# A triangular inverse written earlier into the program, and SBUF pools moved to equal offsets

## The chip, the cores and the metric

The kernel runs on one core of a Trainium2 chip. A core has five engines, each with its own instruction stream: TensorE (PE in the profile; its weight loads are listed apart as PEld), VectorE (DVE), ScalarE (ACT), GpSimd (POOL) and SyncE (SP, which here only issues DMAs). Each engine works through its stream in order, and engines wait for each other on semaphores. Operands live in SBUF (128 partitions), and matmul results in PSUM, in eight banks of 128 x 512 fp32. The metric is the device time in microseconds of one execution.

## The reference: what is computed

Two layers of a diffusion backbone over 512 latent tokens and 256 context tokens with 1024 channels. Layer 0 puts a chunked gating MLP and a bidirectional RWKV-7 mixer with eight heads side by side, between one input projection and one output projection; layer 1 is a bidirectional chunkwise mLSTM. After each mixer comes a ConvFFN: an up projection to 2 x 2816 channels, a 3x3 depthwise convolution, a gated GELU and a down projection. Norms, adaLN modulation, gates and residual adds stand around each part.

The change touches the RWKV-7 recurrence, which the reference writes token by token:

```
def step(s, inp):
    r_t, w_t, k_t, v_t, kk_t, b_t = inp
    sa = jnp.einsum('bhvk,bhk->bhv', s, kk_t)
    s = s * w_t[:, :, None, :] - sa[..., None] * b_t[:, :, None, :] + v_t[..., None] * k_t[:, :, None, :]
    return s, jnp.einsum('bhvk,bhk->bhv', s, r_t)
```

It runs over context, then latent tokens, in both directions. Because each step subtracts what the state already holds along kk, a block of tokens can be done at once only with the inverse of a unit lower triangular matrix between its tokens.

The second thing that the change touches is where the tiles of the later parts lie, ConvFFN included:

```
a, b = jnp.split(h @ w_up, 2, axis=-1)
a = dwconv1d(a, conv_w[1]) if rows is None else dwconv_grid(a, conv_w, rows)
return (jax.nn.gelu(a + conv_b) * b) @ w_down
```

## The kernel before

**Stages.** Norms and adaLN rows of layer 0 (to about 140 us), its projection stage (to about 380), the chain stage of the RWKV recurrence (398 to 615), the output projection (to about 700), ConvFFN 0 (706 to 1236), the mLSTM (to about 1590) and ConvFFN 1 (to the end). Matmuls against weights are done in three passes over a high and a low part of each fp32 operand (`load_w`, L118 to L125, makes the parts: ScalarE rounds to `hi`, VectorE or GpSimd subtracts to get `lo`).

**Sets.** The eight RWKV heads are worked as four pairs of heads, called sets here and numbered ct = 0 to 3 as in the code. For each set, the projection stage makes its inputs (`prep_e`, `prep_n`), stores them to a DRAM area (`setd`, by `set_part`), and inverts its triangular 64 x 64 blocks (`prep_t`, L579 to L636).

**The inverse.** `prep_t` takes the 32 x 32 diagonal blocks by forward substitution on VectorE: 31 steps of two tensor operations each (L597 a product into `fs`, L599 an addition into `Ti`), of up to 256 elements per partition. It gives up control after every third step, that is ten times. Then come three block transposes on VectorE (`Td` L604, `Tn` L605, `On` L607), four copies on ScalarE of 32 x 768 into `TT` (L613, L614), two groups of small matmuls `w` (L621) with copies to `Wm`, two groups `t` (L630) with copies into `TT` on VectorE (L633), and a store of `TT` to DRAM (L636). It yields once behind the copies, and once behind each matmul group, so it consists of 15 pieces and the store. The scratch tiles have one buffer each: `Ai`, `Td` and `Wm` share one, `Ti` and `On` another. So the inverse of a set can begin only when the one before has used up its tiles. Sets 0 and 1 are inverted in the projection stage; sets 2 and 3 are written behind it, and use the single PSUM bank "7".

**The chain stage.** Four lanes, one per set, walk 12 steps each over the tokens. Lanes 0 and 1 run side by side, then lanes 2 and 3. Each group of 4 steps of a lane first loads its part of the set back from DRAM (`rbp`, `LB`, `ttp`, L932 to L943) and is prepared (`prep_g`: transposes, `az` products). The stage is six blocks: blocks 0 to 2 are the three groups of lanes 0 and 1, blocks 3 to 5 those of lanes 2 and 3. Beside the lanes' steps, a block weaves in the preparation of the next group; block 0 the inverse of set 2, block 1 the inverse of set 3 (`inverse()`, which at its end closes the inverse's scratch pool `tx` and opens `late0`, a pool for adaLN rows, in its place); blocks 2 to 4 the job `ada` that multiplies these rows (L157, loads L154). `finish` ends a pair of lanes.

**What sets the order.** `weave` (L302) interleaves generators: it always advances the one whose progress key is least, where a generator with weight w and start f has the key f + (1 - f)(done + 0.5)/w. This fixes the order in which the program writes its instructions. A planner of the framework then simulates the machine and gives each engine an order: among the instructions ready at a time it takes the first written one, except that the lanes' chain steps are written under a raised priority (`crit`). So an instruction written late may run early, where an engine would else be idle. On the chip the resulting order of each engine is strict. DMAs of SP's queue are issued in the same way, in a strict order.

**Pools.** SBUF is handed out from both ends: most pools grow from the left, some (`H`, `act1`, `inv0`, the weights' working tiles of the projection stage) from the right. A pool's start follows from the sizes of those before it. From the pool of the residual stream (`x`, L1142) on, the left pools `xc`, `strm` (split weights), `gatebc`, `strmr` (raw weights), `wo0` to `wo7`, `op0`, and the ConvFFN's `fhid` (hidden tiles, with the convolution's coefficients `fpar`) and `fs` (scratch) follow one another.

Of the kernel before, what the change touches and what calls it, by code (L numbers as in the profile page):

```python
# [8 lines left out]
F32 = mybir.dt.float32  # L9
# [5 lines left out]
P = 128  # L15
# [36 lines left out]
PF = _Cols()  # L52
# [17 lines left out]
def build(tc, *args, **kw):  # L70
    with ExitStack() as ctx:
        _build(ctx, tc, *args, **kw)


def _build(ctx, tc, xall, par, cst, ada_0, ada_w, ada_t, w_in, w_out, ffn_up, ffn_down, lora, wsT, a_bs, c_in, c_gate, c_out, mneg, parf, parm, out):
# [9 lines left out]
    def bank(name, role):  # L85

        turn[role] = turn.get(role, -1) + 1
        return pp.tile([P, 512], F32, tag=role[turn[role] % len(role)], name=name)
# [201 lines left out]
    def woven(*gens):  # L290

        live = [[g[0], 0, g[1], g[2] if len(g) > 2 else 0.0] for g in gens]
        while live:
            k = min(range(len(live)), key=lambda j: live[j][3] + (1 - live[j][3]) * (live[j][1] + 0.5) / live[j][2])
            try:
                next(live[k][0])
                live[k][1] += 1
            except StopIteration:
                live.pop(k)
            yield  # L300

    def weave(*gens):  # L302
        for _ in woven(*gens):
            pass

    def part_of(g, n):
        for _ in range(n):
            next(g)
            yield

    def run(gen):
        for _ in gen:
            pass
# [16 lines left out]
    with ExitStack() as lx:  # L330
# [102 lines left out]
        prbank = lambda name: bank(name, "2435")  # L433
# [9 lines left out]
        def conv_tile(col, pool, tag, name, bufs=1):  # L443
            pl, pcx = unit(col, name)
            y = pool.tile([P, T], F32, tag=tag, name=name, bufs=bufs)
            ci = col - 8
            for (a, n, src) in ((0, TC, pcx), (TC, TL, pl)):
                conv3(y[:, a:a + n], src, pc("shift0", ci), pc("shift1", ci), pc("shift2", ci), n)
            return y
# [19 lines left out]
        def set_part(ct, k):  # L469
            o = 0  # L470
            for kk_, n in SET:
                if kk_ == k:
                    return setd[ct][:, o:o + n]
                o += n
# [78 lines left out]
        def prep_n(ct):  # L553

            s = st[ct]
            RBv = s["RB"].rearrange("p (u a t) -> p u a t", a=2, t=64)
            LBv = s["LB"].rearrange("p (u a t) -> p u a t", a=2, t=64)
            NF = wkT.tile([P, 56, 32], F32, tag="NF", name=f"NF{ct}", bufs=2)
            G.memset(NF[:, 24:32], 0.0)
            G.memset(NF[:, 32:56], 0.0)  # L560
            for g8 in range(3):
                px, py = bank(f"nx{ct}{g8}", "23"), bank(f"ny{ct}{g8}", "45")
                for k in range(8):
                    u = g8 * 8 + k
                    mm(px[0:64, k * 64:k * 64 + 64], LBv[0:64, u, u // 12, :], RBv[0:64, u, 0, :], start=True, stop=True)
                    mm(py[64:128, k * 64:k * 64 + 64], LBv[64:128, u, u // 12, :], RBv[64:128, u, 0, :], start=True, stop=True)
                us = slice(g8 * 8, g8 * 8 + 8)
                for (pp, b0, e) in ((px, 0, A), (py, 64, A)):
                    p3 = pp.rearrange("p (u t) -> p u t", t=64)
                    cpy = e.copy if e is A else e.tensor_copy  # L570
                    off = slice(32 + g8 * 8, 40 + g8 * 8)
                    cpy(NF[b0:b0 + 32, us], p3[b0:b0 + 32, :, 0:32])
                    cpy(NF[b0 + 32:b0 + 64, us], p3[b0 + 32:b0 + 64, :, 32:64])
                    cpy(NF[b0 + 32:b0 + 64, off], p3[b0:b0 + 32, :, 32:64])
                yield
            for k in ("RB", "LB"):
                nc.sync.dma_start(set_part(ct, k), s[k])
            s["NF"] = NF
# [266 lines left out]
        def ada_job(jobs, pool, rawb, *how):  # L845
            for g in jobs:
                yield from ada_gen(g, pool, "7", rawb, *how)

        def kr(ct):
            st[ct] = {}  # L850
            for c0, tag in ((12, "kT"), (8, "rT")):
                st[ct][tag] = conv_tile(c0 + ct, wkP, tag, f"{tag}{ct}", 2)
                yield

        def v(ct):
            st[ct]["vT"] = conv_tile(16 + ct, wkS, "vT", f"vT{ct}")
            yield

        def chained(*gens):
            for g in gens:  # L860
                yield from g

        def start_prep(ct):
            PLt = keep.tile([P, 24], F32, name=f"PL{ct}")
            st[ct]["PL"] = PLt
            for k, n in SET:
                if k not in ("vT", "TT"):
                    st[ct][k] = wkS.tile([P, n], F32, tag=k, name=f"{k}{ct}")
            return prep_e(ct, st[ct]["kT"], st[ct]["rT"])
# [10 lines left out]
        def part(n):  # L880
            for _ in range(n):
                next(SG)
                yield

        NA = (4, 6, 6)
        run(kr(0))
        weave((start_prep(0), 8), (chained(v(0), kr(1), part(0)), 3 + 0))
        run(prep_n(0))
        for ct in range(3):
            n = NA[ct]  # L890
            weave(*([(prep_t(ct, prbank), 13, 0.0)] if ct < 2 else []), (chained(start_prep(ct + 1), prep_n(ct + 1)), 9 + 3, 0.0),
                  (chained(v(ct + 1), *([kr(ct + 2)] if ct < 2 else []), part(n)), 3 + n, 0.0))
        run(SG)
        ex.close()
        hx.close()
        rx.close()
        sx.close()
        Ts = [prep_t(ct, lambda name: bank(name, "7")) for ct in (2, 3)]
        fin = lx.enter_context(tc.tile_pool(name="fin0", bufs=1))
        ch = lx.enter_context(tc.tile_pool(name="chain0", bufs=1))  # L900
        ys = [[fin.tile([P, 2, w], F32, name=f"y{n}{w}") for w in (TC, TL)] for n in ("01", "23")]
# [43 lines left out]
        def load_bv(ct):  # L945
            t = fin.tile([P, T], F32, tag="bv", name=f"bvr{ct}", bufs=2)
            nc.sync.dma_start(t, set_part(ct, "bv"))
            st[ct]["bv"] = t
# [3 lines left out]
        def inverse():  # L952
            yield from Ts[1]
            tx.close()
            late["p"] = lx.enter_context(tc.tile_pool(name="late0", bufs=1))
            nc.scalar.dma_start(lwg, lora[:, 1024:1536])

        def preps(cts, g):
            for ct in cts:
                if g == 0:  # L960
                    load_v(ct)
                load_g(ct, g)
            for ct in cts:
                load_t(ct, g)
                yield from prep_g(ct, g)
# [7 lines left out]
        for b, (k, g) in enumerate(blocks):  # L973
            n = (22, 20, 22 - 10 * k)[g]
            todo = [(part_of(C[k], n) if g < 2 or k else C[k], n)]
            if b < 5:
                kk_, gg_ = blocks[b + 1]
                todo.append((preps(pairs[kk_], gg_), 10))
            if b == 0:
                todo.append((Ts[0], 13))  # L980
            elif b == 1:
                todo.append((inverse(), 13))
            elif b < 5:
                todo.append((part_of(ada, (5, 6, 5)[b - 2]), (5, 6, 5)[b - 2]))
            if b == 3:
                for ct in range(2):
                    load_bv(ct)
                todo.append((finish((0, 1), ys[0], ("01", "01"), "ctx"), 8))
            elif b == 4:
                todo.append((finish((0, 1), ys[0], ("01", "01"), "lat"), 8))  # L990
            elif b == 5:
                todo.append((finish((2, 3), ys[1], ("01", "01"), "ctx"), 8))
            weave(*todo)
            if g < 2:
                run(part_of(C[k], 4))
            if b == 1:
                ada = ada_job([1, 2], late["p"], 2, 2048)
            if b == 2:
                C.append(chains(pairs[1], ys[1]))
            if b == 4:  # L1000
                run(ada)
                gate_rows(0, 0, "7")
                scale_vec(0, 1)
                load_bv(2)
                load_bv(3)
# [53 lines left out]
    def ffn(l, xt, hT, ctx_too, after, final=None, beneath=None):  # L1059

        with ExitStack() as fx:
            hidp = fx.enter_context(tc.tile_pool(name=f"fhid{l}", bufs=1))
            hid = [hidp.tile([P, NH, w], F32, tag=f"hid{g}", name=f"hid{l}{g}") for g, w in ((0, TL), (1, TC))[:2 if ctx_too else 1]]
            fpar = hidp.tile([P, PF.n], F32, name=f"fpar{l}")
            nc.scalar.dma_start(fpar, parf[l])
            sp = fx.enter_context(tc.tile_pool(name=f"fs{l}", bufs=1))
            fill = beneath(sp) if beneath else None
# [71 lines left out]


    strm.sub, strm.hi, strm.lo = nc.vector, 3, 3
    xp = ctx.enter_context(tc.tile_pool(name="x", bufs=1))  # L1142
    H = {tg: ctx.enter_context(tc.tile_pool(name=f"H{tg}", bufs=1, side="right")) for tg in ("lat", "ctx")}
    xcx = ExitStack()
# [56 lines left out]
    def beneath(pool):  # L1201
# [6 lines left out]
        return ada_sums(rows, place)  # L1208

    ffn(0, xt, hT, True, to_layer1, None, beneath)  # L1210


# [396 lines left out]
```

## Time and profile before

| what | value |
|---|---|
| median of three runs | 1970.32 us (1968.26 to 1972.65) |
| the profiled execution | 1975.72 us, with a span of 1973.8 us from the first to the last instruction |
| mean granted TensorE clock | 0.965 of full speed |
| TensorE busy | 1854.0 us, 94% of the span |
| VectorE busy | 1334.4 us, 68% |
| ScalarE busy | 800.1 us, 41% |
| GpSimd busy | 306.9 us, 16% |
| DMA | 227.77 MB, mean 115 GB/s |

How to read the views: a row of the timeline has the start in us, the duration, the engine, the line of the kernel, the operation, the output and input tiles (without set and buffer numbers), the shapes, and how many instructions are drawn together; in brackets stands the idle time of the engine before it and what ended that. A row of a group of instructions has the busy time and the mean duration in ns, then the idle time in front and what ended most of it. In a table of stretches, each engine has its busy time and, in brackets, its instructions; then come the granted clock of TensorE (PEclk, 1.00 is full speed), the share of time that the DMA engines moved data, and their rate. SPq rows are DMA issues on SP's queue.

### The profile page before, as it was taken

The page shows a single profiled execution, that of the slowest core. Times are in us where ns is not written, and L with a number is a line of the kernel's source. Part 1 is how long each engine was busy: PE and PEld are TensorE (multiplying, and loading weights), DVE is VectorE, ACT ScalarE, POOL GpSimd, SP SyncE. Part 2 cuts the span into 40 slices and gives each one's busy share as a digit, 9 for nine tenths or more (in the row PEclk, how much of TensorE's full clock was granted, in tenths as well). Part 3 has the DMA queues.
Part 4 walks back from the last instruction along what each step waited for, and adds up shares of the span by engine and source line. Part 5 has one row for each costly group of instructions (what it writes and reads, how often), then busy time and mean ns, then how long its engine had stood idle before and what let it go on. Part 6 is the DMA issues. An engine that isn't in the chain of part 4 may idle for free.

```text
span 1973.8 us, 31872 instructions
## 1 busy us (share of the span) xinstructions
PE 1854.0 (94%) x12411; PEld 1508.3 (76%) x12411; DVE 1334.4 (68%) x2669; ACT 800.1 (41%) x1429; POOL 306.9 (16%) x429
## 2 busy tenths in 40 slices
PE   6998789698898999999999998999999989999998
PEld 4777677587666888888888886778888768888886
DVE  4379675757345589999994337667777688777534
ACT  4364645534335442222222226475554353323222
POOL 2222222311000222223330002100110020000001
PEclk9999889788899999999999999999999999999999
DMA  7133121643764524444432224431111312222222
GB/s 292 54 123 123 57 103 55 182 123 83 204 184 138 182 99 160 150 160 165 161 134 76 97 96 160 151 92 44 33 43 44 139 56 96 96 96 96 88 94 86
DMA packets 102887, 227.77 MB, mean 115 GB/s; under 512 B 28224, under 2 KB 44048, under 8 KB 99664
## 3 DMA queue, kind: packets, MB, share of 16 engines
q1 hardware_dynamic: 100976, 222.26, 33.4%
q10 hardware_dynamic: 1760, 3.47, 0.5%
q8 instruction: 98, 1.61, 0.3%
q14 instruction: 53, 0.43, 0.1%
HBM read 199.31 MB, written 26.39 MB: 114 GB/s over the span
## 4 chain that ended last, share of the span: by engine, by line
PE 58%; DVE 2%; POOL 1%; ACT 1%; issue 1%; DMA 0%; DVEq 0%; SPq 0%; ACTq 0%; POOLq 0%
PE of L1044 5%; PE of L1043 5%; PE of L1045 5%; PE pl_fb L268 4%; PE pl_fb L266 4%; PE pl_fb L267 4%; PE pl_fa L267 4%; PE pl_fa L268 4%; PE pl_fa L266 4%; PE pd L1453 1%; PE pe L1430 1%; PE kv L1386 1%; PE pc_fa L267 1%; PE pc_fa L266 1%; PE pc_fb L266 1%; PE pc_fb L268 1%
## 5 line engine op out<-in xcount | busy, mean ns | idle before, releaser
L1091 DVE SCALAR_TENSOR_TENSOR cv<-pl_fa,fpar,cv 128x441 f32<-128x441 f32 (+2 forms) x352 | 243.1, 691 | 16.5 <-ACT cv L1080 11.3
L1045 PE MATMUL of<-hi_fd,hlo 128*128 128x512 f32 x440 | 173.4, 396 | 3.0 <-DVE hlo L1115 3.0
L1044 PE MATMUL of<-lo_fd,hhi 128*128 128x512 f32 x440 | 174.6, 397 | 1.4 <-DVE lo_fd L125 1.4
L1043 PE MATMUL of<-hi_fd,hhi 128*128 128x512 f32 x440 | 173.7, 397 | 0.0
L201 DVE SCALAR_TENSOR_TENSOR aj<-am,srb 128x512 f32<-128x512 f32 x224 | 163.3, 729 | 10.0 <-DMA am<-in_ada_t_dram 5.6
L1115 DVE TENSOR_TENSOR hlo<-hid,hhi 128x512 fp32r<-128x512 f32 (+1 forms) x66 | 39.2, 601 | 133.9 <-ACT hhi L1114 133.7
L1114 ACT ACTIVATE hhi<-hid 128x512 fp32r<-128x512 f32 (+1 forms) x66 | 36.7, 559 | 177.2 <-PE of L1044 173.5
L1045 PEld LDWEIGHTS of<-hi_fd,hlo 128*128 128x128 f32 x440 | 83.2, 189 | 22.6 <-DVE hlo L1115 3.4
L1044 PEld LDWEIGHTS of<-lo_fd,hhi 128*128 128x128 f32 x440 | 83.3, 189 | 21.5 <-DVE lo_fd L125 2.3
L125 DVE TENSOR_TENSOR lo_fd<-raw_fd,hi_fd 128x1024 fp32r<-128x1024 f32 x66 | 80.8, 1224 | 26.0 <-ACT hi_fd L124 25.8
L1043 PEld LDWEIGHTS of<-hi_fd,hhi 128*128 128x128 f32 x440 | 83.1, 189 | 19.8 <-ACT hi_fd L124 0.5
L222 POOL TENSOR_SCALAR rstd_p_f<-sq_f,sq_f 128x1 f32<-128x1 f32 x10 | 6.9, 689 | 569.6 <-ACT jk_f L1022 569.6
L124 ACT ACTIVATE hi_fd<-raw_fd 128x1024 fp32r<-128x1024 f32 x66 | 69.2, 1049 | 28.7 <-DMA raw_fd<-in_ffn_down_dram 12.2
L124 ACT ACTIVATE hi_fa<-raw_fa 128x1024 fp32r<-128x1024 f32 x44 | 46.4, 1054 | 79.0 <-PE pl_fb L267 64.4
L124 ACT ACTIVATE hi_fb<-raw_fb 128x1024 fp32r<-128x1024 f32 x44 | 46.7, 1061 | 69.6 <-PE pc_fa L267 38.5
L125 POOL TENSOR_TENSOR lo_fb<-raw_fb,hi_fb 128x1024 fp32r<-128x1024 f32 x22 | 59.4, 2699 | 88.8 <-ACT hi_fb L124 88.8
L125 POOL TENSOR_TENSOR lo_win<-raw_win,hi_win 128x1024 fp32r<-128x1024 f32 x23 | 57.5, 2503 | 90.9 <-ACT hi_win L124 90.0
L1093 ACT ACTIVATE cv<-cv 128x512 f32<-128x512 f32 x44 | 27.8, 632 | 106.7 <-DVE cv L1091 106.7
L267 PE MATMUL pl_fa<-h1f_latlo,hi_fa 128*128 128x512 f32 x176 | 69.6, 396 | 0.0
L266 PE MATMUL pl_fb<-h0f_lathi,hi_fb 128*128 128x512 f32 x176 | 69.6, 396 | 0.0
L268 PE MATMUL pl_fa<-h0f_lathi,lo_fa 128*128 128x512 f32 x176 | 69.6, 395 | 0.0
L267 PE MATMUL pl_fb<-h0f_latlo,hi_fb 128*128 128x512 f32 x176 | 69.5, 395 | 0.0
(695 smaller groups left out, 5507.4 us busy)
## 6 DMA issues: line engine op xcount, KB each, us to landing
raw_fd<-in_ffn_down_dram SPq DMA_DIRECT2D x66, 512.0 KB, 3.2
am<-in_ada_t_dram SPq DMA_DIRECT2D x112, 256.0 KB, 3.0
raw_fa<-in_ffn_up_dram SPq DMA_DIRECT2D x44, 512.0 KB, 3.3
raw_fb<-in_ffn_up_dram SPq DMA_DIRECT2D x44, 512.0 KB, 3.2
raw_win<-in_w_in_dram SPq DMA_DIRECT2D x23, 512.0 KB, 3.3
ada<-in_ada_dram SPq DMA_DIRECT2D x8, 1024.0 KB, 8.9
ada<-in_ada_w_dram SPq DMA_DIRECT2D x8, 1024.0 KB, 8.0
raw_cin<-in_c_in_dram SPq DMA_DIRECT2D x16, 512.0 KB, 3.4
```

What stands on the lines that cost most here:

```text
L124: nc.scalar.activation(hi[:, c], raw[:, c], AF.Copy)
L125: strm.sub.tensor_tensor(lo[:, c], raw[:, c], hi[:, c].bitcast(F32), ALU.subtract)
L201: V.scalar_tensor_tensor(place(f"aj{i}{h}{cnd}", "junk"), raw, 1.0, sb[cnd * 2 + h], ALU.mult, ALU.mult, accum_out=acc[:, cnd, h:h + 1])
L266: mm(p, wh[:, kt, :], hh[:, kt], start=(kt == 0), stop=False)
L267: mm(p, wh[:, kt, :], hl[:, kt], start=False, stop=False)
L268: mm(p, wl[:, kt, :], hh[:, kt], start=False, stop=(kt == KT - 1))
L1043: mm(o[i][hf], hi, w[0][:, c], start=f, stop=False)
L1044: mm(o[i][hf], hi, w[1][:, c], start=False, stop=False)
L1045: mm(o[i][hf], lo, w[0][:, c], start=False, stop=e)
L1091: V.scalar_tensor_tensor(dv, src[:, r0 + dy:r1 + dy, c0 + dx:c1 + dx], fw(ky * 3 + kx), dv, ALU.mult, ALU.add)
L1114: A.activation(hi, hid[cnd][:, k], AF.Copy)
L1115: V.tensor_tensor(lo, hid[cnd][:, k], hi.bitcast(F32), ALU.subtract)
```

## The change

- The generators of sets 2 and 3 (`Ts`) are made ahead of the projection stage. In its last round (ct = 2), where formerly no inverse was woven in, the first 7 pieces of set 2's inverse, that is 21 of its 31 substitution steps, are written with weight 7 and start 0.2.
- Block 0 of the chain stage weaves in what is left of set 2 (8 pieces and the store), and behind it the first 6 pieces of set 3, together with weight 14 (before: all of set 2 with weight 13). Block 1 weaves in the rest of set 3 with weight 9 (before: all of set 3 with weight 13).
- The ConvFFN's coefficient tile `fpar` is padded from 220 columns (NH = 22, ten coefficients each) to 256, of which the first 220 are used. A tile of 32 columns that nothing uses, `gap`, stands ahead of the pool `x`. Both change only where later pools lie.

```diff
         NA = (4, 6, 6)
+        Ts = [prep_t(ct, lambda name: bank(name, "7")) for ct in (2, 3)]
         run(kr(0))
...
-            weave(*([(prep_t(ct, prbank), 13, 0.0)] if ct < 2 else []), (chained(start_prep(ct + 1), prep_n(ct + 1)), 9 + 3, 0.0),
+            weave((prep_t(ct, prbank), 13, 0.0) if ct < 2 else (part_of(Ts[0], 7), 7, 0.2), (chained(start_prep(ct + 1), prep_n(ct + 1)), 9 + 3, 0.0),
                   (chained(v(ct + 1), *([kr(ct + 2)] if ct < 2 else []), part(n)), 3 + n, 0.0))
...
         sx.close()
-        Ts = [prep_t(ct, lambda name: bank(name, "7")) for ct in (2, 3)]
...
             if b == 0:
-                todo.append((Ts[0], 13))
+                todo.append((chained(Ts[0], part_of(Ts[1], 6)), 14))
             elif b == 1:
-                todo.append((inverse(), 13))
+                todo.append((inverse(), 9))
...
-            fpar = hidp.tile([P, PF.n], F32, name=f"fpar{l}")
+            fpar = hidp.tile([P, 256], F32, name=f"fpar{l}")[:, :PF.n]
...
     strm.sub, strm.hi, strm.lo = nc.vector, 3, 3
+
+    ctx.enter_context(tc.tile_pool(name="gap", bufs=1)).tile([P, 32], F32, name="gap")
     xp = ctx.enter_context(tc.tile_pool(name="x", bufs=1))
```

The helper `part_of(g, n)` (L306) advances a generator by n pieces and leaves the rest of it for later; `chained` runs generators one behind the other.

## The prediction

> **What bounds the kernel now.** I read the page first (span, busy shares), then a table of seven stretches, then the timelines of the engines in the stretches where TensorE falls short.
>
> ```profile
> span 1973.8 us, 31872 instructions
> PE 1854.0 (94%) x12411; PEld 1508.3 (76%) x12411; DVE 1334.4 (68%) x2669; ACT 800.1 (41%) x1429; POOL 306.9 (16%) x429
> core 0: us, PE busy (x) PEld busy (x) DVE busy (x) ACT busy (x) POOL busy (x), PEclk, DMA share, GB/s
> 310.00:380.00 70.00, 55.26 (x445) 43.64 (x444) 55.16 (x105) 37.36 (x80) 18.37 (x20) 0.86 0.28 103
> 400.00:438.00 38.00, 37.90 (x754) 32.87 (x751) 17.15 (x55) 11.93 (x36) 4.74 (x11) 0.92 0.35 98
> 438.00:480.00 42.00, 39.25 (x798) 34.60 (x797) 37.77 (x122) 14.41 (x44) 8.46 (x17) 0.95 0.41 111
> 480.00:531.00 51.00, 41.62 (x633) 30.85 (x630) 18.48 (x49) 21.37 (x40) 1.61 (x4) 0.77 0.56 161
> 710.00:1000.00 290.00, 290.00 (x1660) 253.63 (x1659) 278.95 (x647) 77.38 (x110) 81.94 (x117) 1.00 0.47 161
> 1010.00:1200.00 190.00, 190.00 (x914) 157.77 (x914) 90.70 (x142) 56.40 (x81) 13.32 (x15) 1.00 0.27 94
> 1600.00:1960.00 360.00, 360.00 (x1551) 291.83 (x1550) 230.79 (x295) 113.22 (x140) 0.86 (x2) 1.00 0.26 90
> 480.00:500.00 20.00, 15.58 (x263) 12.99 (x260) 7.82 (x16) 11.42 (x17) 0.00 (x0) 0.57 0.15 41
> 500.00:515.00 15.00, 13.58 (x231) 10.66 (x227) 6.50 (x20) 3.91 (x10) 0.48 (x2) 1.00 0.79 269
> 515.00:531.00 16.00, 12.46 (x144) 7.20 (x145) 4.16 (x13) 6.04 (x13) 1.13 (x3) 0.79 0.86 208
> ```
>
> In the three long stretches of the two ConvFFNs (from 710 on) TensorE is busy all the time at clock 1.00: nothing but fewer or shorter matmuls shortens them. The early chain stage, 400 to 480, is nearly as full. The one stretch in the reach of this change where TensorE both idles and loses its clock is 480 to 531, and its bad parts are 480 to 500 and 515 to 531. So the question is what stands there, and whether the change moves it.
>
> **The substitution's first part: where the trace has it already.** Set 2 is the third pair of heads, set 3 the fourth.
>
> ```profile
> 314.42 2.26 DVE L633 COPY TT<-t 32x512 f32<-32x512 f32 x4 [16.81 <-PE t L630]
> 318.49 2.07 DVE L585 STREAM_TRANSPOSE Ai<-NF 128x1024 f32<-128x1024 f32 x1
> 376.94 0.19 DVE L599 TENSOR_TENSOR Ti<-Ti,fs 128x31 f32<-128x31 f32 x1
> 378.44 1.54 ACT L613 COPY TT<-Td 32x768 f32<-32x768 f32 x1 [5.88 <-DVE Td L604]
> 433.44 1.38 DVE L633 COPY TT<-t 32x512 f32<-32x512 f32 x2 [2.00 <-PE t L630]
> 437.10 0.85 DVE L633 COPY TT<-t 32x256 f32<-32x256 f32 x2 [0.69 <-PE t L630]
> 437.97 1.96 DVE L585 STREAM_TRANSPOSE Ai<-NF 128x1024 f32<-128x1024 f32 x1
> L599 DVE TENSOR_TENSOR Ti<-Ti,fs 128x31 f32<-128x31 f32 (+15 forms) x31 | 10.9, 351 | 0.3
> L597 DVE TENSOR_TENSOR fs<-Ai,Ti 128x31 f32<-128x31 f32 (+15 forms) x31 | 10.7, 346 | 0.4
> ```
>
> The program writes set 2's substitution behind the whole projection stage, yet its first instruction ran at 318.49 and its last at 376.94: the planner issued it early as filler in VectorE's gaps (14.8 of 70 us idle between 310 and 380). It cannot begin earlier, since its buffers (one of each) are held by set 1 until the copies at 314.42. Writing 21 of the 31 steps into the stage therefore changes ranks among instructions that run there anyway. I price it at 0, by that cover; a step moved ahead of projection work could hold it up by a few 0.35 us operations (+2), an earlier end could save 1: bounds -1 and +2.
>
> **What does move.** With 7 of its 15 pieces written earlier, set 2's remaining 8 pieces lead a chain of 14 in block 0 of the chain stage, where all 15 formerly shared that block by weight 13. Its two groups of t matmuls, formerly the pieces 14 and 15 (0.96 and beyond the block's end by weight), come at about 7.5/14 = 0.54 at the latest. Block 0 spans about 398 to 438, so its last copy moves from 437.10 to about 418. Set 3 waits for exactly these buffers (its transpose stands 0.02 us behind that copy, 437.97), so it may start some 18 us earlier. The last two rows, groups of VectorE between 437 and 480, price its steps: 10.9 + 10.7 = 21.6 us in 62 operations. VectorE is idle for 38 - 17.15 = 20.85 us in 400 to 438, about half of it behind 418: ten of the 21.6 us fit there. The other 12 then fall into 438 to 480, where VectorE's remaining work is 37.77 - 21.6 - 2.0 (transpose) = 14 of 42 us, so a third of the time is taken: 12/0.67 = 18, an end near 457 to 464 in place of 479. No instruction and no DMA is added. VectorE runs in order, so each 0.35 us step may stand ahead of a chain copy that TensorE waits for, now in 418 to 438 as well: I take +1 (0 to +2) since TensorE idles only 2.75 of 42 us in the stretch where steps do that now.
>
> **What stands behind the late end.** The next rows are the tail of set 3 and those queued behind it.
>
> ```profile
> 481.25 1.50 ACT L613 COPY TT<-Td 32x768 f32<-32x768 f32 x1
> 485.81 1.49 ACT L614 COPY TT<-Td 32x768 f32<-32x768 f32 x1
> 487.32 0.27 ACT L710 COPY Qs<-c 128x128 f32<-128x128 f32 x1
> 482.71 0.43 PE L691 MATMUL c<-W,AZ 128*64 128x64 f32 x4 [1.70 <-DVE AZ L672]
> 484.33 0.31 PE L621 MATMUL w<-TT,On 32*32 32x32 f32 x2 [1.18 <-ACT TT L614]
> 487.35 1.91 PE L621 MATMUL w<-TT,On 32*32 32x32 f32 x62 [1.48 <-ACT TT L614]
> 497.47 1.38 DVE L633 COPY TT<-t 32x512 f32<-32x512 f32 x2 [7.01 <-PE t L630]
> 502.15 0.34 SPq L154 DMA_DIRECT2D ada<-in_ada_w_dram  x1
> 502.95 0.33 SPq L636 DMA_DIRECT2D setd<-TT  x1
> 503.33 6.62 SPq L154 DMA_DIRECT2D ada<-in_ada_w_dram  x2
> 510.40 2.56 SPq L943 DMA_DIRECT2D ttp<-setd  x4
> 523.25 0.34 PE L739 MATMUL y<-AZ,W 128*64 128x64 f32 x4 [2.04 <-ACT W L719]
> 524.74 0.69 PE L725 MATMUL c<-W,LT 128*64 128x64 f32 x8 [1.15 <-DVE W L720]
> ```
>
> Piece one, 480 to 500: four copies of 1.5 us hold ScalarE from 481.25 to 487.30, the lanes' Qs copy comes right behind them, TensorE waits three times (1.70, 1.18, 1.48) and runs at clock 0.57. Piece two, 500 to 531: set 3's result is stored at 502.95 and loaded again at 510.40 behind two ada loads of SP's queue, so lane 3 starts late and TensorE waits 2.04 and 1.15 us at 523 to 525.
>
> The prices, against the stretch 438 to 480 with its 2.75 idle us in 42 (0.065 per us) and clock 0.95. Piece one: idle 20 - 15.58 = 4.42, less 1.31, is 3.1 us; if all its busy time scaled with the clock, 15.58 x (0.95 - 0.57) = 5.9 us more. Bounds 3.1 and 9.0. Piece two: idle (15 - 13.58) + (16 - 12.46) = 4.96, less 31 x 0.065 = 2.0, is 2.9; with clock 12.46 x (0.95 - 0.79) = 2.0 more: 2.9 and 4.9.
>
> Piece two should go whole: block 1 gives the tail a weight of 9 instead of 13, so the copies fall near its middle and the store comes some 20 us before lane 3 wants it, ahead of the ada loads in SP's queue (they wait for that tail too, through the pool that takes its place). I take -3.9, the middle. Piece one doesn't go, it moves to about 460 to 468: the same 6 us of copies, with both lanes and the next group's preparation to fill TensorE. I take half of its middle, -3.0 (all to none: -9 to 0).
>
> The Trainium skill, "TensorE: Matmul & The Clock Gate", section "What's actually happening", has the clock halve after an idle window of about 3.4 us. The trace disagrees here: the longest wait at 480 to 488 is 1.70 us and the clock falls to 0.57. By the page, copies that only make short waits would cost no clock at 460, and the sum would be about 3 us lower; by the trace they do, and the measurement decides.
>
> **The offsets.** fpar grows from 220 to 256 columns and a 128-byte tile stands ahead of the x pool. By the compiled layout of before, most left-side pools behind it (the streamed weights, x, the ConvFFN's hidden tiles) start at 352 past a multiple of 512 bytes, the ConvFFN's scratch at 224, the right-side pools at 480; both edits bring all to 480. Rows of one operation at both offsets (raw_win, hi_win at 480, the others at 352):
>
> ```profile
> L124 ACT ACTIVATE hi_fa<-raw_fa 128x1024 fp32r<-128x1024 f32 x44 | 46.4, 1054 | 79.0 <-PE pl_fb L267 64.4 <-PE pc_fb L267 6.2 <-DMA raw_fa<-in_ffn_up_dram 5.0
> L124 ACT ACTIVATE hi_win<-raw_win 128x1024 fp32r<-128x1024 f32 x23 | 24.1, 1057 | 21.1 <-PE pc_u L267 6.6 <-issue 5.3 <-PE pc_kT L267 2.7
> raw_fa<-in_ffn_up_dram SPq DMA_DIRECT2D x44, 512.0 KB, 3.3
> raw_win<-in_w_in_dram SPq DMA_DIRECT2D x23, 512.0 KB, 3.3
> L267 PE MATMUL pl_fa<-h1f_latlo,hi_fa 128*128 128x512 f32 x176 | 69.6, 396 | 0.0
> ```
>
> 1054 against 1057 ns, 3.3 against 3.3 us: nothing. I price the offsets at 0, with TensorE full over them. For the worse: VectorE's 278.95 of 290 us would have to grow by over 4% to pass TensorE, and 5% makes 292.9, so +3 (+4 with the smaller stages). For the better: the cover holds unless the matmuls themselves shorten; one in a hundred over these 840 us would be -8.
>
> **The sum.** 0 + 1 - 3.9 - 3.0 + 0 = -5.9 us. The profiled execution took 1975.72 us, 1.9 around its span, and would become 1969.8. It stood 5.4 us above the median of the three runs, 1970.32, in which the same stalls should stand; so the forecast for the median is 1964.4 us, its own range 1959 to 1968.
>
> **The rivals.**
> No effect (1969.5, chance 0.23): lane 3's wait is replaced by the group loads (DMA share 0.79 and 0.86 in 500 to 531) and piece one lands elsewhere whole; for it speaks that TensorE's 1854 busy us don't change; against it that the store at 502.95 is so plainly late. This is also what "the third pair begun earlier" comes to if its early part was all the edit did.
> Slower (1975, chance 0.17): the copies stand in mid-block ahead of ScalarE's Qs and W copies of both lanes while VectorE has substitution steps in front of the lanes' copies too. The whole of piece one then recurs with twice as many lane steps queued: 9.0 where it was 9.0, plus as much clock again over the 14 us behind it (13 x 0.38 = 5), plus 2 from VectorE, less piece two at its smallest, 2.9: about +4 to +5. It decides if the clock between 455 and 475 falls below 0.7. Against it: in 438 to 480 ScalarE is busy 14.41 of 42 us, with room.
> Slower by the offsets (1973, chance 0.04): VectorE above 290 us in the 710 to 1000 stretch.
> Faster by the offsets (1956, chance 0.07): matmuls 1% shorter on top of the forecast. The equal rows above speak against it.
>
> **How the numbers follow.** The forecast has the remaining 0.49. A measurement of this kernel can tell about 0.2%, 3.9 us. Of the forecast's 0.49 some 0.08 falls inside that, so faster is 0.41 + 0.07 = 0.48 and, with 0.04 where piece one goes whole in the no-effect case, 0.52; same is 0.23 - 0.04 + 0.08 = 0.27; slower 0.17 + 0.04 = 0.21. The range must hold 8 in 10 and reach both to the slower case and to the gain with all of piece one (-9 - 4.9 = -13.9, 1956) and some of the offsets: 1953 to 1976.
>
> **What would show it.** Right: set 3's transpose of Ai near 418 to 422, its last step before 465, its store before 490, lane 3's first W copy without the wait at 523, and 480 to 531 with a clock above 0.9. Set 2's last step still near 377. Rows of L124, L125 and the matmuls within 1% of before. Wrong: set 3 starting still near 438; the clock low between 455 and 475; a new wait of SP's queue ahead of lane 3; or the ConvFFN's stretches, full before, changed in length.

## The result, and the profile after

The changed kernel takes **1953.94 us** (median of seven runs, 1948.68 to 1960.66) against 1970.32 us (1967.37 to 1974.81): 16.4 us less, a ratio of **0.9918**, 95% interval 0.9898 to 0.9939. The forecast was 1964.4 us, its range 1953 to 1976. The time lies just inside the range, the sign is right, and the reason is mostly wrong: nearly all of the gain comes from the part that I priced at nothing.

The profiled execution took 1960.66 us. First its page, with the span and the busy shares:

```profile
span 1958.8 us, 31874 instructions
PE 1838.4 (94%) x12411; PEld 1511.1 (77%) x12411; DVE 1332.7 (68%) x2669; ACT 800.5 (41%) x1429; POOL 306.4 (16%) x429
```

TensorE has the same 12411 matmuls, but is busy for 1838.4 us instead of 1854.0. Where the stretches are full of matmuls, that is a shorter time for each. The table of stretches of the kernel before, for ConvFFN 1 (200 us of its up projection, 80 us of its down projection; behind the busy time stands the number of matmuls):

```profile
1600.00:1800.00 200.00, 200.00 (x862) 162.12 (x861) 156.94 (x208) 66.77 (x79) 0.00 (x0) 1.00 0.26 93
1860.00:1940.00 80.00, 80.00 (x346) 64.87 (x345) 28.13 (x30) 23.45 (x30) 0.00 (x0) 1.00 0.26 92
```

The same stretches of the kernel after:

```profile
1600.00:1800.00 200.00, 200.00 (x884) 165.65 (x883) 159.93 (x210) 66.37 (x79) 0.00 (x0) 1.00 0.28 98
1860.00:1940.00 80.00, 80.00 (x355) 66.24 (x354) 27.33 (x29) 22.16 (x28) 0.00 (x0) 1.00 0.24 86
```

Both times TensorE is full at clock 1.00, and 884 matmuls go through where 862 did, 355 where 346 did. 200 us by 862 and by 884 are 232 and 226 ns. Taken from the starts of successive 128x512 matmuls, the step is 232.4 ns before and 226.7 ns after (means over these stretches, as are the steps of the up and down projections below). One line's view in the same 80 us shows what changed about it. Before (minimum, median and maximum of the duration):

```profile
L1043 PE MATMUL of<-hi_fd,hhi x116: 390/393/404, 1859.7 to 1939.9; 128*128 128x512 f32 x116
```

After:

```profile
L1043 PE MATMUL of<-hi_fd,hhi x119: 389/389/389, 1859.7 to 1939.9; 128*128 128x512 f32 x119
```

Before, the durations scatter from 390 to 404 ns; the steps run through 228 to 241 ns in a pattern that repeats every seven matmuls. After, every one is the same. The duration hides the size of it, since matmuls overlap: it falls by 4 ns, the step by 5.7.

The chain stage, where I looked for the gain, is as long as before. From the first chain matmul to the first one of the output projection it takes 236.6 us before (390.6 to 627.2; the 398 to 615 in the list of stages is too short) and 238.3 after; from there to the end 1346.6 and 1333.0. So the later stages shortened by 13.6 us and the chain stage by nothing; what stands ahead of the chain stage (390.6 and 387.4 us) varies from 381 to 391 us over all profiled executions, also where its instructions are the same.

### The profile page after: what moved, and what is told of

Its sections match the earlier page's. It is cut to its first block, busy times and chain, and to the rows that moved or that the text cites. A ratio compares the mean times of both kernels' runs of the same rounds, so it can differ in the third digit from the quotient of the medians.

```text
span 1958.8 us, 31874 instructions
## 1 busy us (share of the span) xinstructions
PE 1838.4 (94%) x12411; PEld 1511.1 (77%) x12411; DVE 1332.7 (68%) x2669; ACT 800.5 (41%) x1429; POOL 306.4 (16%) x429
## 4 chain that ended last, share of the span: by engine, by line
PE 58%; DVE 2%; POOL 1%; ACT 1%; issue 1%; DMA 1%; POOLq 0%; DVEq 0%; ACTq 0%; SPq 0%
PE of L1044 5%; PE of L1043 5%; PE of L1045 5%; PE pl_fb L266 4%; PE pl_fb L267 4%; PE pl_fb L268 4%; PE pl_fa L267 4%; PE pl_fa L266 4%; PE pl_fa L268 4%; PE pd L1455 1%; PE pe L1432 1%; PE pc_fa L268 1%; PE pc_fb L268 1%; PE pc_fb L267 1%; PE pc_fa L267 1%; PE pc_fb L266 1%
## 5 line engine op out<-in xcount | busy, mean ns | idle before, releaser
L124 ACT ACTIVATE hi_fa<-raw_fa 128x1024 fp32r<-128x1024 f32 x44 | 46.4, 1055 | 77.3 <-PE pl_fb L267 62.5
L266 PE MATMUL pl_fa<-h0f_lathi,hi_fa 128*128 128x512 f32 x176 | 69.2, 393 | 0.0
L267 PE MATMUL pl_fa<-h0f_latlo,hi_fa 128*128 128x512 f32 x176 | 69.1, 392 | 0.0
```

Of the source, the lines that this page charges most:

```text
L124: nc.scalar.activation(hi[:, c], raw[:, c], AF.Copy)
L266: mm(p, wh[:, kt, :], hh[:, kt], start=(kt == 0), stop=False)
L267: mm(p, wh[:, kt, :], hl[:, kt], start=False, stop=False)
```

## The experiments

All kernels start from the kernel before. Two theories stood against each other at first: A, the offsets shorten the matmuls; B, the order brings the gain. The differences below are those of the starts of a matmul's two operands in SBUF: the one that is streamed (512 columns) less the one that is held (128 x 128), modulo 256 bytes. In the up projections the activations are streamed and the weights held; in the down projections and the output projection it is the other way round. All starts are those of the compiled layouts.

**The offsets alone** (e1).

```diff
-            fpar = hidp.tile([P, PF.n], F32, name=f"fpar{l}")
+            fpar = hidp.tile([P, 256], F32, name=f"fpar{l}")[:, :PF.n]
...
+    ctx.enter_context(tc.tile_pool(name="gap", bufs=1)).tile([P, 32], F32, name="gap")
```

> The offsets alone (gap and the padded fpar), the order of the work as before. Theory A, the long matmuls read their two operands faster when both start at the same place within 512 bytes: steps of the 128x512 matmuls fall from 232.4 to 227 ns from the output projection on, the stages there shorten by 13 to 14 us as in the trace of after (up 0 by 3.0, down 0 by 2.0, up 1 by 5.8, down 1 by 3.0), median 1957. Theory B, the offsets do nothing and the changed order brings the gain: 1970, steps 232.

Measured: 1955.0 us, ratio 0.9916 (0.9889 to 0.9943), the whole gain. Steps 226.7 ns; from the output projection to the end 1332.5 us.

**The order alone** (e2): the change without these two edits.

> The order alone (first pieces of set 2 in the projection stage, the new weights), all pools where they were. Theory A: the chain stage ends 2 to 3 us earlier and nothing else moves, median 1968, steps 232. Theory B: 1954. My forecast for this part was 1964.4.

Measured: 1970.89 us, ratio 0.9995 (0.9978 to 1.0012), steps 232.4 ns, chain stage 235.1 us. Nothing that can be told from no change. Theory B is out. The first stretch of e1 and that of e2:

```profile
1600.00:1800.00 200.00, 200.00 (x884) 165.62 (x883) 158.73 (x209) 66.14 (x79) 0.00 (x0) 1.00 0.29 98
1600.00:1800.00 200.00, 200.00 (x863) 162.11 (x862) 157.15 (x205) 63.75 (x77) 0.00 (x0) 1.00 0.30 97
```

**Each of the two offset edits** (e3 the gap, e4 the padded fpar).

> The gap of 128 bytes alone: streamed weights at 480 like the activations on the right side (up projections and output projection equal), the ConvFFN's scratch at 352 against weights at 480 (down projections unequal by 128, as before). Theory A: up and output projection 227 ns, down still 232, 1970 - 13.5 + 5 = 1962. Theory B: 1970.

> The padded fpar alone: the scratch moves from 224 to 352, equal to the streamed weights at 352, but not at 480; the up projections stay unequal (352 against 480). Theory A in the form that only equality counts: down 227 ns, up 232, 1970 - 5 = 1965. Theory A in the form that the operands must start at 480: down 232, 1970.

Measured: e3 1958.19 us, ratio 0.9933 (0.991 to 0.9957); e4 1967.68 us, ratio 0.9981 (0.9965 to 0.9997). The table of stretches, e3:

```profile
1600.00:1800.00 200.00, 200.00 (x884) 165.62 (x883) 159.34 (x210) 66.56 (x79) 0.00 (x0) 1.00 0.29 98
1860.00:1940.00 80.00, 80.00 (x346) 64.87 (x345) 25.23 (x27) 22.53 (x32) 0.86 (x2) 1.00 0.24 79
```

And e4:

```profile
1600.00:1800.00 200.00, 200.00 (x863) 162.16 (x862) 157.50 (x206) 64.16 (x76) 0.00 (x0) 1.00 0.29 96
1860.00:1940.00 80.00, 80.00 (x355) 66.24 (x354) 28.79 (x30) 23.66 (x30) 0.00 (x0) 1.00 0.26 86
```

With the gap alone, the up projection is fast (884) and the down projection slow (346); with fpar alone, it is the other way round (863 and 355). In e4 both operands of the down projection start at 352 within 512 bytes and not at 480, so it isn't a certain place that helps, but that the two are equal. Together the two edits cover all three matmul groups.

**Other differences** (e5, e6, e7): the sizes of fpar and of the gap varied. e5 is shown; e6 has 264 and 96 columns, e7 272 and 64.

```diff
-            fpar = hidp.tile([P, PF.n], F32, name=f"fpar{l}")
+            fpar = hidp.tile([P, 240], F32, name=f"fpar{l}")[:, :PF.n]
...
+    ctx.enter_context(tc.tile_pool(name="gap", bufs=1)).tile([P, 24], F32, name="gap")
```

> Offsets of other differences, order as before: a gap of 96 bytes and fpar of 240 columns put the streamed weights at 448 (the activations on the right stay at 480, so the up projections differ by 32) and the scratch at 384 (down projections differ by 64). If only exact equality helps: 232 ns in both, 1970. If the loss grows with the difference: steps between 227 and 232 in both, nearer to 227 in the up projections, 1960 to 1966.

> A gap of 384 bytes and fpar of 264 columns: streamed weights at 224 (up projections differ by 256), scratch at 256 (down projections differ by 32, scratch above the weights). If equality within 256 bytes is enough: up 227 ns, down 232, 1962. If it must be within 512: 232 ns in both, 1970.

> Differences of the other sign: a gap of 256 bytes and fpar of 272 columns put the streamed weights at 96 (up projections: activations at 480, that is 128 above within 256) and the scratch at 160 (down projections differ by 64, scratch above the weights). Theory, only a difference of 0 within 256 bytes is fast: 232 to 234 ns in both, 1968 to 1971. Rival, the sign decides (scratch above the weights is harmless): down at 227, 1965.

Measured: e5 1967.95 us, ratio 0.9984 (0.9967 to 1.0); e6 1957.7 us, 0.9942 (0.992 to 0.9964); e7 1973.65 us, 1.0017 (1.0004 to 1.003). The same two stretches of e5, e6 and e7:

```profile
1600.00:1800.00 200.00, 200.00 (x859) 160.67 (x858) 155.86 (x204) 65.15 (x77) 0.00 (x0) 1.00 0.29 95
1860.00:1940.00 80.00, 80.00 (x352) 65.62 (x351) 27.43 (x29) 22.17 (x28) 0.00 (x0) 1.00 0.27 92
```

```profile
1600.00:1800.00 200.00, 200.00 (x884) 165.64 (x884) 158.54 (x209) 66.87 (x79) 0.00 (x0) 1.00 0.28 96
1860.00:1940.00 80.00, 80.00 (x345) 64.40 (x343) 24.91 (x26) 22.16 (x31) 0.80 (x2) 1.00 0.23 79
```

```profile
1600.00:1800.00 200.00, 200.00 (x862) 162.14 (x862) 154.78 (x202) 65.78 (x78) 0.00 (x0) 1.00 0.28 96
1860.00:1940.00 80.00, 80.00 (x345) 64.45 (x344) 27.55 (x29) 23.66 (x30) 0.00 (x0) 1.00 0.27 93
```

The steps, from the starts of the matmuls, sorted by the difference modulo 256 bytes:

| difference, bytes | where | step, ns |
|---|---|---|
| 0 | e1, e3 up, e4 down, e6 up, e12 all | 226.7 |
| 32 | e5 up | 233.3 |
| 64 | e5 down | 228.9 |
| 128 | before, up and down; e7 up | 232.4 |
| 192 | e7 down | 233.3 |
| 224 | e6 down | 233.3 |

In e6 the up projection's operands differ by 256 bytes and are as fast as with no difference. The loss doesn't grow with the difference: 32 bytes cost more than 64. So e5's expectation of a graded loss fell, and so did its other one, 232 ns in both, since 64 bytes cost only 2.2 ns. In e7 the sign doesn't decide, and the kernel is a little slower than before. The table's 232.4 and 233.3 can't be told apart by the difference alone: in e9 (below), whose operands lie as before, the down projection's step is 233.3 too.

**Equal within 256, not within 512, in the up and output projections** (e12): gap of 96 columns, fpar of 256.

> Order as before, a gap of 384 bytes and fpar of 256 columns: weights and scratch both at 224, the right-side pools at 480; nothing is equal within 512 bytes between the sides, everything within 256. Theory, 256 bytes is the period: steps 227 everywhere, 1955 as with the change's own offsets. Rival, the period is 512 for some of the pairs: output and up projections at 232, 1965.

Measured: 1956.43 us, ratio 0.9931 (0.9912 to 0.9949), steps 226.7 ns in the up and down projections and 226.9 in the output projection (645 to 690 us). The prediction counts starts within 512 bytes; for the up and output projections 256 are enough. The down projection's operands both start at 224 here, so they are equal within 512 as well.

**The projection part of the order alone** (e10).

```diff
-                todo.append((chained(Ts[0], part_of(Ts[1], 6)), 14))
+                todo.append((Ts[0], 6, 0.5385))
...
-                todo.append((inverse(), 9))
+                todo.append((inverse(), 13))
```

(against e2's kernel)

> Of the order alone the projection part: 7 pieces of set 2 written in the projection stage, its remaining pieces at their former places in block 0 (weight 6, start 0.5385), block 1 as before. My step, these instructions ran there anyway: 1970 to 1971, VectorE's order in the projection stage unchanged, set 3's start at 47 us behind the first chain matmul as before. Rival, writing them early helps by itself: 1967 or less.

Measured: 1966.87 us, ratio 0.9989 (0.9975 to 1.0003). The median touches the rival's 1967, but the interval holds no change, so the time alone leaves it open whether there are 2 us in it. In e10 as in e2, VectorE's and ScalarE's instructions of the last 70 us ahead of the chain stage stand in exactly the order of before. Behind that, in the first 55 us of e10's chain stage, the order differs in places. Set 3 starts 45.1 us behind the first chain matmul, against 47.3 before, and the chain stage takes 233.2 us, against 236.0 to 237.1 in the eight profiled executions with the former order (before, e1, e3 to e7, e12). Their clock from 20 to 50 us behind the first chain matmul is 0.85 to 0.89, e10's is 0.94:

```profile
402.80:432.80 30.00, 29.70 (x612) 26.46 (x611) 18.07 (x52) 8.83 (x27) 4.09 (x9) 0.94 0.39 113
```

That speaks for some 3 us. It is a single profiled execution, though, and e2 and the changed kernel, whose order in the chain stage is nearly the same, lie 3.2 us apart (235.1 and 238.3).

**What the late inverse costs at all** (e8, e9).

```diff
-            for s_ in range(31):
+            for s_ in range(31 if ct < 3 else 0):
```

> Set 3's 31 substitution steps are left out (its inverse stays the unit matrix, so lane 3 computes with other numbers); all copies, matmuls, stores and loads of its tail stay and come some 25 to 30 us earlier than in the kernel before. Theory P, the late tail costs the 6.0 to 13.9 us that I read out of 480 to 531: 1956 to 1965. Theory Q, the chain stage as a whole is bound by TensorE's work and the tail's waits only move: 1968 to 1971.

Measured: 1967.49 us, ratio 0.9982 (0.9971 to 0.9994), chain stage 231.5 us. Set 3's tail ran some 33 us earlier than before (its copies 57 us behind the first chain matmul, against 90), and that, with the 21.6 us of VectorE's work that go, is worth 3.3 us by the medians, 3.5 by the ratio: short of theory P's range, and half a us beyond Q's.

```diff
-                    nc.sync.dma_start(tt[hsl[h], d, :, h], set_part(ct, "TT").rearrange("p (u t) -> p u t", t=64)[hsl[h], u0:u0 + 4])
+                    nc.sync.dma_start(tt[hsl[h], d, :, h], set_part(ct if ct < 3 else 1, "TT").rearrange("p (u t) -> p u t", t=64)[hsl[h], u0:u0 + 4])
...
-            yield from Ts[1]
+            for _ in range(15):
+                yield
```

> Set 3's inverse is left out whole (lane 3 loads set 1's result): no substitution, no copies, no w and t matmuls, no store. Theory P: the stall of 6.0 to 13.9 us and some 5 us of TensorE work go, 1951 to 1959. Theory Q: only TensorE's own work for it goes, some 5 us, 1965. Either way it bounds from above what any new place of this inverse can bring.

Measured: 1956.28 us, ratio 0.9933 (0.9909 to 0.9956), chain stage 219.0 us. Without any of set 3's inverse the kernel gains 13 us by the ratio (9 to 18), inside P's range and more than Q's 5. That is its work and its waits together, so an upper bound for any new place of it. e8, which keeps the tail and only moves it, gains 3.5; the other 10 us or so go with the copies, matmuls and store that e8 still has.

**Where the gain of the order went.** The stretches of the chain stage, cut at the same distances from its first chain matmul (20, 50, 80, 110, 145, 205, 232 us; columns as in the prediction's table). Before, from 20 on:

```profile
410.60:440.60 30.00, 29.91 (x565) 26.54 (x563) 16.59 (x48) 7.20 (x22) 3.53 (x8) 0.85 0.33 101
440.60:470.60 30.00, 28.46 (x592) 25.07 (x590) 26.21 (x84) 11.73 (x36) 7.25 (x14) 0.98 0.50 126
470.60:500.60 30.00, 24.37 (x457) 20.96 (x459) 17.37 (x52) 13.18 (x24) 1.21 (x3) 0.72 0.10 28
500.60:535.60 35.00, 29.97 (x458) 20.61 (x456) 11.70 (x38) 11.08 (x28) 2.21 (x6) 0.90 0.88 241
535.60:595.60 60.00, 58.74 (x856) 38.70 (x852) 27.98 (x80) 19.54 (x47) 4.21 (x11) 1.00 0.65 191
595.60:622.60 27.00, 22.28 (x374) 16.18 (x368) 15.45 (x52) 13.14 (x30) 1.61 (x4) 1.00 0.11 36
```

The order alone (e2):

```profile
401.10:431.10 30.00, 29.48 (x426) 24.14 (x424) 14.66 (x43) 5.96 (x18) 4.20 (x8) 0.72 0.20 59
431.10:461.10 30.00, 28.38 (x596) 25.30 (x593) 27.76 (x92) 10.32 (x32) 5.43 (x12) 1.00 0.51 134
461.10:491.10 30.00, 25.91 (x545) 22.37 (x539) 17.11 (x48) 13.93 (x27) 2.02 (x5) 0.89 0.30 77
491.10:526.10 35.00, 33.55 (x610) 25.32 (x611) 14.16 (x48) 12.20 (x36) 3.14 (x8) 1.00 0.92 275
526.10:586.10 60.00, 56.04 (x795) 35.65 (x795) 27.89 (x81) 21.11 (x49) 4.00 (x9) 1.00 0.58 163
586.10:613.10 27.00, 21.11 (x316) 15.19 (x312) 13.35 (x43) 13.68 (x29) 1.21 (x3) 1.00 0.16 49
```

TensorE's idle time (length less busy) in the stretch of lane 3's late start falls from 35 - 29.97 = 5.03 to 1.45 us, and around the copies from 5.63 to 4.09: the stalls that I had read did go, 5.1 us in all. But in the last two stretches it grows from 1.26 + 4.72 = 5.98 to 3.96 + 5.89 = 9.85, so 3.9 us come back. And the clock is better around the copies (0.89 for 0.72), but worse where set 2's w and t matmuls now stand (0.72 for 0.85, with 426 matmuls done there instead of 565). What makes lanes 2 and 3 end no earlier, though they begin earlier, I didn't separate by a run; e8 shows the same idle time at the end (27 us with 21.15 busy).

## Why the prediction was right or wrong

**The projection part, 0 (-1 to +2): right for the projection stage, open behind it.** The instructions stood there already, in the same order. Set 2's Td transpose lies 13.3 us ahead of the first chain matmul in e2, 13.5 before. But with this part alone (e10) set 3 started 2.2 us earlier and the chain stage of the profiled execution was 3 us shorter, which my working had no term for; the ratio (5 us faster to 0.6 slower) leaves the size open.

**"Its last copy moves from 437.10 to about 418": failed.** Rows of the kernel after:

```profile
418.01 1.38 DVE L633 COPY TT<-t 32x512 f32<-32x512 f32 x2 [3.38 <-PE t L630]
425.84 0.85 DVE L633 COPY TT<-t 32x256 f32<-32x256 f32 x2 [2.64 <-PE t L630]
427.11 1.97 DVE L585 STREAM_TRANSPOSE Ai<-NF 128x1024 f32<-128x1024 f32 x1
```

Only the first of the two copy groups stands at 418; the second needed another 8 us, since TensorE, at half clock there (0.50 from 418 to 426), took the t matmuls in pieces between chain matmuls. (By weight both groups stood beyond the block's end before, at 13.5/13 and 14.5/13; the 0.96 was miscounted, which changes nothing here.) Set 3 starts at 427.11, and 39.7 us behind the first chain matmul against 47.3 before: 8 us earlier, not 18. So the "ten of the 21.6 us" that should have been done ahead of 438 were not (3.1 us were, six of the 31 steps), and counted from the first chain matmul the tail came 4.5 to 7.5 us earlier instead of 15 to 22.

**Piece two, -3.9: right in its stretch, lost by the end.** Lane 3's wait of 2.04 and 1.15 us is gone and the stretch gained 3.6 us of idle time. The error is one of kind: I counted an idle time that goes as time won, without asking what the lanes behind it run into. **Piece one, -3.0: mis-sized.** It gained 1.5 us of idle time at its place, and the clock there rose from 0.72 to 0.89, but the stretch of set 2's t matmuls fell from 0.85 to 0.72. My sign for both pieces, a clock above 0.9 from 480 to 531, came true all the same:

```profile
480.00:531.00 51.00, 48.35 (x944) 38.25 (x940) 21.02 (x68) 15.30 (x46) 3.54 (x9) 0.91 0.73 206
```

TensorE idles 2.65 us there instead of 9.38, and the chain stage is no shorter: a sign taken from one stretch doesn't show a gain of the whole stage. e8 bounds both pieces together: 3.5 us (1.2 to 5.7) where I had 6.9 for a smaller move, and a lower bound of 6.0 that I took for safe.

**SP's queue: earlier, but not in the order that I forecast.** The store still waited for the tail, and an ada load still stands ahead of it; both are 11 us earlier.

```profile
491.43 0.34 SPq L154 DMA_DIRECT2D ada<-in_ada_w_dram  x1
492.24 0.33 SPq L636 DMA_DIRECT2D setd<-TT  x1
501.88 2.71 SPq L943 DMA_DIRECT2D ttp<-setd  x4
```

I had put the store "before 490" and ahead of the ada loads; it is neither, and lane 3 was in time all the same.

**The offsets, 0 (-8 for one in a hundred): failed, and this is the step that made the result.** The cover that I named was right, with its condition: "the cover holds unless the matmuls themselves shorten". They did, by 5.7 of 232.4 ns, 2.5%, and with that a sign of being right failed (matmuls within 1%) and one of being wrong came: the ConvFFN's full stretches changed in length. The reading behind the zero was wrong in two ways. I compared ScalarE's and the DMA's rows at both offsets (they stayed: 1054 and 1055 ns for hi_fa, 3.3 and 3.4 us for raw_fa), but put one TensorE row beside them with nothing to compare it to. And I looked at each operand's own offset, where the pair matters. The trace of before held the answer. One row of its projection stage, where both operands start at 480, would have done:

```profile
L267 PE MATMUL pl_kT<-h_latlo,hi_win 128*128 128x512 f32 x32 | 12.5, 391 | 0.0
```

That is 391 ns beside the 396 of pl_fa. Other rows of that stage have longer means (412 for the same line's pl_u), because part of their matmuls ran at half clock, which hides the difference in a view of durations. The steps show it: 228.4 ns in the projection stage, without those at half clock (some 427 ns), and 232.4 in the ConvFFN, at a granted clock of 1.00 throughout.

**The rivals.** "Faster by the offsets", 1956 us at a chance of 0.07, named the mechanism and comes within 2.1 us of the time: its 1% for the matmuls was too little, and the forecast's 5.9 us for the order, which it added, too much. "No effect" describes the order's half. The mid-block rival didn't come: the clock from 452 to 480 stayed near full.

```profile
452.00:466.00 14.00, 13.11 (x252) 11.71 (x252) 12.95 (x41) 4.85 (x15) 3.74 (x8) 1.00 0.53 137
466.00:480.00 14.00, 9.95 (x187) 8.21 (x187) 9.97 (x28) 9.46 (x16) 1.21 (x3) 0.98 0.32 88
```

"VectorE above 290 us" didn't come either:

```profile
710.00:1000.00 290.00, 290.00 (x1674) 256.78 (x1673) 281.06 (x651) 77.67 (x110) 85.80 (x120) 1.00 0.47 161
```

VectorE is at 281.06 us (290 would have needed just under 4% more than before, not over 4%), and its cover grew thinner by what TensorE now does more in the same time.

## What to carry to other kernels

Where TensorE is full, read the step between matmul starts and not the duration alone, and compare it between stages at the same granted clock: here two stages with the same shape and another step differed in where their operands start. Then line up where the streamed and the held operand of the long matmuls start, modulo 256 bytes; here a tile of 128 bytes ahead of a pool and 144 more in another did it, at no cost in instructions. And an idle time that a new order takes away is won only if the end of the stage moves: cut both traces at the same distances from the stage's start, and sum the idle time over the whole stage.

## What the runs showed of the hardware

The step of a 128x512 matmul depends on where its two operands start relative to each other: 226.7 ns at a difference of 0 modulo 256 bytes, 228.9 at 64, 232.4 or 233.3 at 128, 233.3 at 32, 192 and 224. The matmuls of 256 columns in ConvFFN 0 behave otherwise: 119.0 ns at 128, 119.7 at 0 and 117.3 at 32. Why, no run here shows. The Trainium skill, "TensorE: Matmul & The Clock Gate", section "Step-by-step: what each phase is for", has TensorE read the streamed and the held operand through two ports, so that loading the next weights takes nothing from the running matmul. A step that depends by up to 3% on how the two starts lie to each other doesn't fit that; the measurement decides, though no run separates the weight load from the streaming.

The granted clock can fall while the profile shows no idle time of TensorE. In the kernel after:

```profile
412.00:425.00 13.00, 13.00 (x141) 9.60 (x137) 2.69 (x8) 1.26 (x4) 0.40 (x1) 0.60 0.01 3
```

13.00 of 13 us busy, 141 small matmuls, clock 0.60: t matmuls of 32 columns between chain matmuls of 64, and some matmuls of 128. The idle window of about 3.4 us, behind which the Trainium skill, "TensorE: Matmul & The Clock Gate", section "What's actually happening", has the clock halve, isn't in this stretch of the profile. The ends of matmuls are modelled there, so short gaps between small ones may not show.
